# Key loads moved from SyncE's hardware queue to GpSimd's software queue, and state rows the other way

## The chip, the core and the metric

The kernel runs on one core of one Trainium2 chip. The core's engines work side by side: TensorE (PE in the profile, its weight loads PEld), VectorE (DVE), ScalarE (ACT), GpSimd (POOL) and SyncE (SP). SP computes nothing here; it only starts data transfers. Transfers run on 16 shared DMA engines. A transfer started by SP goes through queue q1, whose descriptors are made in hardware; one started by GpSimd goes through queue q0, whose descriptors GpSimd writes in software (the page calls the two kinds "hardware_dynamic" and "software_dynamic"). The metric is device time in microseconds (us) of the one core, taken without the profiler; the profile is one execution of its own.

## What is computed

For 16 sequences of 2048 steps with 256 channels, the reference runs this recurrence for every channel. It is the numerically safe form of a weighted mean over the past, with decay `w` per step and a bonus `u` for the current step:

```python
for t in range(seq_len):
    kk = k[b, t, :].copy()
    vv = v[b, t, :].copy()
    ww = u + kk
    qq = np.maximum(pp, ww)
    e1 = np.exp(pp - qq)
    e2 = np.exp(ww - qq)
    output[b, t, :] = (e1 * aa + e2 * vv) / (e1 * bb + e2 + 1e-08)
    ww = pp - w + kk
    qq = np.maximum(ww, kk)
    e1 = np.exp(ww - qq)
    e2 = np.exp(kk - qq)
    aa = e1 * aa + e2 * vv
    bb = e1 * bb + e2
    pp = qq
```

`k`, `v` and the output have 16 x 2048 x 256 float32 numbers, 33.55 MB each.

## The kernel before

The time axis is cut into a head of 32 steps and 16 stages of 126 steps. In a stage, the steps lie on the partitions and the recurrence becomes matrix products with triangular matrices. The unit of work is a **pair**: four sequences of one stage, 126 steps x 4 x 256 numbers. There are 64 such pairs (16 stages x 4), and two smaller ones for the head, which are put third and fourth: 66 pairs in all, numbered n = 0 to 65.

One pair takes these operations, by line:

- `load` (L121; L115 for the head): one transfer of 512 KB for `k` into a tile `kr` and one for `v` into a tile `vr`. Each tile has four buffers.
- `round_k` (L258, DVE): casts `kr` into `km`, a float32r matrix that also holds rows with `w` and `u`. `logs` (L266, PE): `km` times two matrices gives the exponents X in PSUM. `exps` (L277, ACT): their exponentials, into the tile `ez`.
- `cast_v` (L285, DVE): `vr` to bfloat16 `vb`. `times_v` (L293, DVE): `ez` times `vb`.
- `sums` (L323, PE): sums over the steps of a stage, for the state.
- `den` (L457, PE), `recip` (L465 and L466, ACT), `num` (L475, PE), `mult` (L483, DVE): denominator, its reciprocal, numerator, and the product, into the tile `rd`.
- `store` (L499, GpSimd; L494 for the head): one transfer of 504 KB from `rd` to the output.

Once per stage, a chain of small operations carries the state from stage to stage (L332 to L424; on DVE among others the copy of the sums L346, the copy L364, then L366 to L368, L387 to L392, L402, L404 and L417). It ends in `inject`: DVE copies the new state into a small tile `row` (L429), and four transfers of 8 KB put it into partitions 126 and 127 of the `ez` tiles of that stage (L433, issued by GpSimd), where the `den` and `num` of the stage's pairs read it.

The main loop has one **slot** per pair, and the order of work on every engine is written out by hand: a helper `K` pins each instruction behind the one before it on its engine. Slot n issues the load of pair n + 3, then the exponentials of pair n, `round_k` of pair n + 1, the output work (`num`, `den`, `recip`, `mult`) of pairs ten or eleven slots back with the store, `times_v` of pair n, `logs` and `cast_v` of pair n + 1. A stage's state is injected at the end of the third slot after its last pair, three slots before the first `den` that reads it. After the last pair, eleven slots only finish outputs.

SP has nothing else to do than loads, in the order k, v, k, v, so it runs ahead of the slots: each load starts as soon as its buffer is free, and a buffer is free when the cast that reads it (`round_k` or `cast_v`) has ended four pairs earlier. GpSimd does its setup work in the first microseconds and afterwards only issues stores and state rows; it waits for the second `mult` of a pair before its store.

Of the kernel before, what the change touches and what calls it, by code (L numbers as in the profile page):

```python
# [22 lines left out]
def kernel(  # L23
# [11 lines left out]
    def K(ins):  # L35

        block, e, new = nc.cur_bb.bb, ins.ins.engine, []
        for i in reversed(block.instructions):
            if i.engine == e:
                new.append(i)  # L40
                if i.name == pinned.get(e):
                    break
        for a, b in zip(new[1:], new):
            tc.add_manual_dep(b, a.name, mybir.DependencyInfo(
                mybir.DependencyClass.NoSync, mybir.DependencyReason.DATA), reason="order")
        pinned[e] = new[0].name
        return ins

    PE, DVE, SC, POOL, SP = nc.tensor, nc.vector, nc.scalar, nc.gpsimd, nc.sync
# [3 lines left out]
    TC = 2 * HS  # L53
# [3 lines left out]
    GB = T0  # L57
    NG = 3
    NH = NG * GB
    AHEAD = 3  # L60
    LAG = 10
    RS = 2.0 ** -43
    LNRS = 43 * 0.6931471805599453
    CAP = 68.0

    consts = ctx.enter_context(tc.tile_pool(name="consts", bufs=1))
    kpool = ctx.enter_context(tc.tile_pool(name="kpool", bufs=AHEAD + 1))
    vpool = ctx.enter_context(tc.tile_pool(name="vpool", bufs=AHEAD + 1))
    vbpool = ctx.enter_context(tc.tile_pool(name="vbpool", bufs=2))
    ezpool = ctx.enter_context(tc.tile_pool(name="ezpool", bufs=7))  # L70
    rpool = ctx.enter_context(tc.tile_pool(name="rpool", bufs=5))
# [15 lines left out]
    NP = len(pairs)  # L87
    kr_of, vr_of = {}, {}

    def is_head(n):  # L90
        return pairs[n][0] < 0

    def tiles_of(n):
        return 1 if pairs[n] == (-1, 1) else 2
# [6 lines left out]
    def load(n):  # L101
        kr = kpool.tile([128, 4, Dm], F32, tag="kr", name="kr")
        vr = vpool.tile([128, 4, Dm], F32, tag="vr", name="vr")
        kr_of[n], vr_of[n] = kr, vr
        c, p = pairs[n]
        if is_head(n):
            if p == 1:
                K(POOL.memset(kr[64:96, 0:2, :], 0.0))
                K(POOL.memset(vr[64:96, 0:2, :], 0.0))
            for t, x in ((kr, k), (vr, v)):  # L110
                for g in range(NG):
                    b = 6 * g + 4 * p
                    e = min(b + 2 * tiles_of(n), B)
                    if b < e:
                        K(SP.dma_start(out=t[g * GB:(g + 1) * GB, 0:e - b, :],  # L115
                                        in_=x[b:e, 0:T0, :].rearrange("n t d -> t n d")))
        else:
            t0 = T0 + c * TC
            r = min(128, T - t0)
            for t, x, eng in ((kr, k, SP), (vr, v, SP if n else SC)):  # L120
                K(eng.dma_start(  # L121
                    out=t[0:r, :, :], in_=x[4 * p:4 * p + 4, t0:t0 + r, :].rearrange("n t d -> t n d")))

# [5 lines left out]
    for n in range(2):  # L129
        load(n)  # L130
# [54 lines left out]
                               -0.5 * HS, op=ALU.mult))  # L185
    fill(NLE[0:HS, TC:TC + 1], 0.5)
    K(DVE.scalar_tensor_tensor(NLE[:, TC + 1:128], cc[:, 2:3], -0.5 * HS, cc[:, 4:5], ALU.mult, ALU.add))
    for n in range(2, AHEAD + 1):
        load(n)
    kms = [consts.tile([128, 4, Dm], F32R, tag=f"km{j}", name=f"km{j}") for j in range(2)]  # L190
    for t in kms:
# [55 lines left out]
    EZ, X_of, KM = {}, {}, {}  # L247

    def round_k(n):
        r = NH if is_head(n) else TC  # L250
        i = 2 * tiles_of(n)
        if is_head(n):
            KM[n] = rpool.tile([128, 2, D], F32, tag="rd", name="kmh").rearrange(
                "p i (n d) -> p (i n) d", n=2).bitcast(F32R)
            K(SC.activation(KM[n][96:98], crow[96:98], ACT.Copy))
        else:
            KM[n] = kms[n % 2]
        K(DVE.tensor_copy(KM[n][0:r, 0:i, :], kr_of.pop(n)[0:r, 0:i, :]))  # L258
# [14 lines left out]
    def exps(n):  # L273
        if n % 2 == 0:
            EZ[n // 2] = ezpool.tile([128, 4, 4, D], BF16, tag="ez", name="ez")
        i = tiles_of(n)
        K(SC.activation(ez_of(n)[:, 0:4:2], X_of.pop(n)[:, :, 0:i, :], ACT.Exp))  # L277
# [26 lines left out]
    def group_of(c, j):  # L304
        return 2 * j if c == 0 else 1 + 2 * c + j
# [6 lines left out]
    def sums(n):  # L312
        c = step_of(n)
        head = c < 0
        if n == first_of[c]:
            TOT[c] = psn.tile([128, D], F32, tag="num", name="num")[0:48] if head else pst.tile(
                [48, D], F32, tag="tot", name="tot")
        for i in range(tiles_of(n)):
            for q in range(2):
                x = 2 * pairs[n][1] + i  # L320
                m = ((OHE, OHV), (OHhE, OHhV))[head][q][:, 8 - x:56 - x]
                r = (NH + NG if head else 128) if q == 0 else (NH if head else TC)
                K(PE.matmul(TOT[c], m[0:r, :], ez_of(n)[0:r, q, i, :],  # L323
                            start=n == first_of[c] and i == 0 and q == 0,
                            stop=n == last_of[c] and i == tiles_of(n) - 1 and q == 1,
                            skip_group_check=True))
# [100 lines left out]
    def inject(c):  # L427
        row = small.tile([128, 128], BF16, tag="row", name="row")
        K(DVE.tensor_copy(row, st.pop((c, "d"))[:, 0:128]))  # L429
        for j in range(2):  # L430
            for h in range(2):
                p = 64 * h + 32 * j
                K(POOL.dma_start(out=EZ[group_of(c, j)][TC + h:TC + h + 1, 0:2, :, :].rearrange(  # L433
                                   "o q i (x c) -> o (q i x) c", c=128),
                               in_=row[p:p + 32, :]))

# [5 lines left out]
    def widen():  # L442
        first_phase.close()
        for name, bufs in (("den", 1), ("num", 2)):
            wide.append(ctx.enter_context(tc.tile_pool(name="wide" + name, bufs=bufs, space=bass.MemoryType.PSUM)))
# [6 lines left out]
    def den(n):  # L452
        rl, ri = (NH, NH) if is_head(n) else (128, TC)
        d = bank("den", [128, 2, D])
        for m, r, q in (((Lh if is_head(n) else Lf), rl, 0), (Id, ri, 2)):
            for i in range(tiles_of(n)):
                K(PE.matmul(d[:, i, :], m[0:r, :], ez_of(n)[0:r, q, i, :], start=q == 0, stop=q == 2,  # L457
                            skip_group_check=True))
        DEN[n] = d

    def recip(n):
        r = NH if is_head(n) else TC
        i = tiles_of(n)
        rd = rpool.tile([128, 2, D], F32, tag="rd", name="rd")
        K(SC.activation(rd[0:r, 0:i, :], DEN.pop(n)[0:r, 0:i, :], ACT.Ln, scale=RS))  # L465
        K(SC.activation(rd[0:r, 0:i, :], rd[0:r, 0:i, :], ACT.Exp, scale=-1.0))  # L466
        RD[n] = rd

    def num(n, i):
        if i >= tiles_of(n):  # L470
            return
        rl, ri = (NH, NH) if is_head(n) else (128, TC)
        d = bank("num", [128, D])
        for m, r, q in (((LhN if is_head(n) else LfN), rl, 1), (IdN, ri, 3)):
            K(PE.matmul(d, m[0:r, :], ez_of(n)[0:r, q, i, :], start=q == 1, stop=q == 3,  # L475
                        skip_group_check=True))
        NUM[n, i] = d

    def mult(n, i):
        if i >= tiles_of(n):  # L480
            return
        r = NH if is_head(n) else TC
        K(DVE.tensor_mul(RD[n][0:r, i, :], NUM.pop((n, i))[0:r, :], RD[n][0:r, i, :]))  # L483
# [34 lines left out]
    def small_work(n, where):  # L518
        for f, c in later.pop((n, where), []):
            f(c)  # L520
# [12 lines left out]
    for n in range(NP + LAG + 1):  # L533
        q, qp = out_at.get(n), out_at.get(n - 1)
        live, out_q, out_qp = n < NP, q is not None, qp is not None
        if n == NP:
            widen()
        if 0 < n and n + AHEAD < NP:
            load(n + AHEAD)
        small_work(n, "first")  # L540
        if live:
            exps(n)
        small_work(n, "exp")
        if 0 < n <= NP:
            sums(n - 1)
        if n + 1 < NP:
            round_k(n + 1)
        small_work(n, "sums")
        if out_qp:
            num(qp, 0)  # L550
            if not live:
                num(qp, 1)
        if out_q:
            den(q)
            recip(q)
        if out_qp:
            mult(qp, 0)
            if live:
                num(qp, 1)
        small_work(n, "pool")  # L560
        if live:
            times_v(n)
        if out_qp:
            mult(qp, 1)
            store(qp)
        if n + 1 < NP:
            logs(n + 1)
            cast_v(n + 1)
        small_work(n, "dve")
        small_work(n, "act")  # L570
        small_work(n, "last")
# [31 lines left out]
```

## Time and profile before

Five runs of the kernel: 350.89, 352.67, 353.19, 353.79 and 355.10 us, median 353.19. The profiled execution is the slowest of them.

| | profiled execution |
|---|---|
| its own time | 355.10 us |
| its span, first to last instruction | 353.4 us |
| DVE busy | 297.1 us, 84% |
| PE busy | 289.5 us, 82% |
| ACT busy | 278.7 us, 79% |
| POOL busy | 99.7 us, 28% |
| stores L499 on POOL | 64, mean 916 ns each |
| state rows L433 on POOL | 64, mean 520 ns each |
| store, issue to landing | median 7.5 us |
| state row, issue to landing | median 7.1 us |
| read from and written to HBM | 68.22 MB and 33.55 MB |

How to read it: "busy" counts the time in which an engine executed something. GpSimd's busy time here is the time in which it writes descriptors, not the transfer itself. The kernel has three phases. It starts up until about 80 us (the pipeline of ten slots fills), it then repeats a steady pattern of four slots, one stage, every 18.66 us until about 310 us, and it drains until 353 us. In a timeline line of the profile, the columns are start in us, length in us, engine, line, operation, tile written <- tiles read, and count.

### The profile page before, as it was taken

The page shows a single profiled execution, that of the slowest core. Times are in us where ns is not written, and L with a number is a line of the kernel's source. Part 1 is how long each engine was busy: PE and PEld are TensorE (multiplying, and loading weights), DVE is VectorE, ACT ScalarE, POOL GpSimd, SP SyncE. Part 2 cuts the span into 40 slices and gives each one's busy share as a digit, 9 for nine tenths or more (in the row PEclk, how much of TensorE's full clock was granted, in tenths as well). Part 3 has the DMA queues.
Part 4 walks back from the last instruction along what each step waited for, and adds up shares of the span by engine and source line. Part 5 has one row for each costly group of instructions (what it writes and reads, how often), then busy time and mean ns, then how long its engine had stood idle before and what let it go on. Part 6 is the DMA issues. An engine that isn't in the chain of part 4 may idle for free.

```text
span 353.4 us, 4174 instructions
## 1 busy us (share of the span) xinstructions
PE 289.5 (82%) x1183; PEld 139.4 (39%) x1200; DVE 297.1 (84%) x636; ACT 278.7 (79%) x286; POOL 99.7 (28%) x164
## 2 busy tenths in 40 slices
PE   0568877788979898988989898979797989887970
PEld 0225433343435444444444353535343544433320
DVE  2566787889999999999999999999999999986451
ACT  2474557779988889898989898888988889977790
POOL 5000006131414141514132231405141405142531
PEclk9975889999999999999999999999999999999895
DMA  7898768699999999999999999999999999634574
GB/s 213 198 352 279 221 224 249 205 326 301 311 354 332 369 313 366 304 360 317 355 328 340 354 334 330 329 336 337 345 335 350 319 313 287 200 123 148 182 237 138
DMA packets 81366, 102.59 MB, mean 290 GB/s; under 512 B 5504, under 2 KB 73152, under 8 KB 81344
## 3 DMA queue, kind: packets, MB, share of 16 engines
q1 hardware_dynamic: 68160, 67.58, 60.2%
q0 software_dynamic: 12496, 34.11, 27.8%
q10 hardware_dynamic: 688, 0.66, 0.8%
q8 instruction: 9, 0.15, 0.2%
q14 instruction: 13, 0.11, 0.1%
HBM read 68.22 MB, written 33.55 MB: 288 GB/s over the span
## 4 chain that ended last, share of the span: by engine, by line
PE 38%; DVE 27%; issue 5%; DMA 4%; ACT 2%; POOL 0%; POOLq 0%; DVEq 0%
PE num L475 11%; PE X L266 9%; DVE rd L483 8%; PE den L457 7%; PE tot L323 7%; DVE ez L293 5%; DVE km L258 4%; DMA ez<-row 4%; PE den L339 4%; DVE vb L285 2%; DVE AB L392 2%; DVE da L391 1%; DVE S L366 1%; ACT rd L466 1%; ACT rd L465 1%
## 5 line engine op out<-in xcount | busy, mean ns | idle before, releaser
L277 ACT ACTIVATE ez<-X 128x2048 bf16<-128x2048 f32 x66 | 122.2, 1852 | 23.4 <-PE X L266 23.4
L499 POOL DMA_DIRECT2D out_dram<-rd x64 | 58.6, 916 | 197.4 <-DVE rd L483 69.5
L483 DVE TENSOR_TENSOR rd<-num,rd 126x512 f32<-126x512 f32 (+1 forms) x131 | 88.5, 682 | 14.5 <-ACT rd L466 7.0
L293 DVE TENSOR_TENSOR ez<-ez,vb 126x2048 bf16<-126x2048 bf16 (+1 forms) x66 | 79.7, 1208 | 8.0 <-ACT ez L277 6.6
L465 ACT ACTIVATE rd<-den 126x1024 f32<-126x1024 f32 (+1 forms) x66 | 66.7, 1011 | 20.7 <-PE den L457 20.7
L466 ACT ACTIVATE rd<-rd 126x1024 f32<-126x1024 f32 (+1 forms) x66 | 69.5, 1053 | 2.1
L266 PE MATMUL X<-km,NLE 128*128 128x512 f32 x128 | 54.4, 508 | 16.2 <-DVE km L258 13.1
L475 PE MATMUL num<-ez,LfN 128*128 128x512 bf16 x127 | 49.0, 386 | 21.4 <-DVE rd L483 20.8
L323 PE MATMUL tot<-ez,OHV 126*48 126x512 bf16 x128 | 49.8, 389 | 8.5 <-DVE ez L293 8.5
L258 DVE CAST km<-kr 126x1024 fp32r<-126x1024 f32 x64 | 50.6, 790 | 5.0 <-ACT km L192 5.0
L323 PE MATMUL tot<-ez,OHE 128*48 128x512 bf16 x128 | 50.8, 397 | 0.0
L475 PE MATMUL num<-ez,IdN 126*128 126x512 bf16 (+1 forms) x131 | 50.3, 384 | 0.2 <-issue 0.2
L285 DVE CAST vb<-vr 126x1024 bf16<-126x1024 f32 (+1 forms) x66 | 44.6, 676 | 3.3 <-DMA vr<-in_v_dram 3.3
L433 POOL DMA_DIRECT2D ez<-row x64 | 32.9, 520 | 47.1 <-DVE km L258 47.1
L266 PE MATMUL X<-km,NLZ 128*128 128x512 f32 x128 | 42.1, 412 | 0.0
L457 PE MATMUL den<-ez,Id 126*128 126x512 bf16 (+1 forms) x131 | 40.0, 386 | 0.9
L266 PEld LDWEIGHTS X<-km,NLE 128*128 128x128 f32 x128 | 24.9, 202 | 29.7 <-DVE km L258 10.0
L457 PE MATMUL den<-ez,Lf 128*128 128x512 bf16 x112 | 35.1, 383 | 1.3 <-DMA ez<-row 1.3
L475 PEld LDWEIGHTS <-IdN 126*128 126x128 bf16 (+1 forms) x131 | 12.8, 98 | 40.4 <-issue 39.2
L266 PEld LDWEIGHTS X<-km,NLZ 128*128 128x128 f32 x128 | 25.7, 201 | 6.2
L323 PEld LDWEIGHTS <-OHE 128*48 128x48 bf16 x128 | 13.2, 103 | 32.8 <-issue 25.7
L475 PEld LDWEIGHTS <-LfN 128*128 128x128 bf16 x128 | 12.4, 97 | 31.7 <-issue 23.2
(95 smaller groups left out, 199.7 us busy)
## 6 DMA issues: line engine op xcount, KB each, us to landing
out_dram<-rd POOLq DMA_DIRECT2D x64, 504.0 KB, 7.5
kr<-in_k_dram SPq DMA_DIRECT2D x60, 512.0 KB
vr<-in_v_dram SPq DMA_DIRECT2D x59, 512.0 KB
kr<-in_k_dram SPq DMA_DIRECT2D x4, 504.0 KB
vr<-in_v_dram SPq DMA_DIRECT2D x4, 504.0 KB
ez<-row POOLq DMA_DIRECT2D x64, 8.0 KB, 7.1
vr<-in_v_dram ACTq DMA_DIRECT2D x1, 512.0 KB
kr<-in_k_dram SPq DMA_DIRECT2D x3, 128.0 KB
```

Source lines behind the costliest of these rows:

```text
L258: K(DVE.tensor_copy(KM[n][0:r, 0:i, :], kr_of.pop(n)[0:r, 0:i, :]))
L266: K(PE.matmul(X[:, q, i, :], m[0:kr, :], km[0:kr, i, :], start=True, stop=True))
L277: K(SC.activation(ez_of(n)[:, 0:4:2], X_of.pop(n)[:, :, 0:i, :], ACT.Exp))
L285: K(DVE.tensor_copy(vb[0:r, 0:i, :], vr_of.pop(n)[0:r, 0:i, :]))
L293: K(DVE.tensor_mul(ez[0:r, 1:4:2], ez[0:r, 0:4:2], vb[0:r, 0:i, :].unsqueeze(1).broadcast_to([r, 2, i, D])))
L323: K(PE.matmul(TOT[c], m[0:r, :], ez_of(n)[0:r, q, i, :], start=n == first_of[c] and i == 0 and q == 0, stop=n == last_of[c] and i == tiles ...
L457: K(PE.matmul(d[:, i, :], m[0:r, :], ez_of(n)[0:r, q, i, :], start=q == 0, stop=q == 2, skip_group_check=True))
L465: K(SC.activation(rd[0:r, 0:i, :], DEN.pop(n)[0:r, 0:i, :], ACT.Ln, scale=RS))
L466: K(SC.activation(rd[0:r, 0:i, :], rd[0:r, 0:i, :], ACT.Exp, scale=-1.0))
L475: K(PE.matmul(d, m[0:r, :], ez_of(n)[0:r, q, i, :], start=q == 1, stop=q == 3, skip_group_check=True))
L483: K(DVE.tensor_mul(RD[n][0:r, i, :], NUM.pop((n, i))[0:r, :], RD[n][0:r, i, :]))
L499: K(POOL.dma_start(out=out[4 * p:4 * p + 4, t0:t0 + TC, :].rearrange("n t d -> t n d"), in_=o[0:TC, :, :]))
```

## The change

The loads of `k` are issued by GpSimd instead of SP, from pair 5 on. The loads of `v` stay on SP. The four transfers of state rows per stage are issued by SP instead of GpSimd. The load of a pair is written four slots ahead of the pair instead of three; the number of buffers stays at four (it was `AHEAD + 1` with `AHEAD = 3` and is `AHEAD` with `AHEAD = 4`). Pairs 0 to 3 are loaded before the loop, as before; pair 4 is now loaded in slot 0 instead of slot 1.

```diff
-    AHEAD = 3
+    AHEAD = 4
...
-    kpool = ctx.enter_context(tc.tile_pool(name="kpool", bufs=AHEAD + 1))
-    vpool = ctx.enter_context(tc.tile_pool(name="vpool", bufs=AHEAD + 1))
+    kpool = ctx.enter_context(tc.tile_pool(name="kpool", bufs=AHEAD))
+    vpool = ctx.enter_context(tc.tile_pool(name="vpool", bufs=AHEAD))
...
-            for t, x, eng in ((kr, k, SP), (vr, v, SP if n else SC)):
+            for t, x, eng in ((kr, k, SP if n <= AHEAD else POOL), (vr, v, SP if n else SC)):
                 K(eng.dma_start(
                     out=t[0:r, :, :], in_=x[4 * p:4 * p + 4, t0:t0 + r, :].rearrange("n t d -> t n d")))
...
-    for n in range(2, AHEAD + 1):
+    for n in range(2, AHEAD):
         load(n)
...
-                K(POOL.dma_start(out=EZ[group_of(c, j)][TC + h:TC + h + 1, 0:2, :, :].rearrange(
+                K(SP.dma_start(out=EZ[group_of(c, j)][TC + h:TC + h + 1, 0:2, :, :].rearrange(
                                    "o q i (x c) -> o (q i x) c", c=128),
                                in_=row[p:p + 32, :]))
...
-        if 0 < n and n + AHEAD < NP:
+        if n + AHEAD < NP:
             load(n + AHEAD)
```

The instructions of PE, DVE and ACT and their order stay as they were. On GpSimd, the order from pair 4's output on becomes: store, k load, store, k load. On SP, it becomes: four v loads, four state rows, four v loads.

## The prediction

> **What bounds the kernel now.** I read the 40-slice rows first, then busy time by stretch, then the waits, then DVE against POOL in the timeline. The page:
>
> ```profile
> DVE  2566787889999999999999999999999999986451
> ...
> DMA  7898768699999999999999999999999999634574
> ...
> q1 hardware_dynamic: 68160, 67.58, 60.2%
> q0 software_dynamic: 12496, 34.11, 27.8%
> ```
>
> Two resources are at 9 from about 80 to 300 us: DVE and the DMA engines. Busy time by stretch, columns stretch, length, busy time of PE, PEld, DVE, ACT, POOL with counts, granted clock, DMA share, GB/s:
>
> ```profile
> 20.00:80.00 60.00, 48.57 (x172) 24.12 (x174) 45.03 (x103) 37.94 (x41) 10.18 (x15) 0.83 0.82 262
> 105.00:305.00 200.00, 180.70 (x776) 88.41 (x787) 191.64 (x386) 178.40 (x182) 62.05 (x87) 1.00 1.00 333
> ```
>
> In the steady part DVE works 191.6 of 200 us and the DMA share reads 1.00. Which one binds? The list of waits of the whole span decides (engine, line, releaser: us in total, times, longest):
>
> ```profile
> DVE vb L285 <- DMA vr<-in_v_dram: 3.3, 1, 3.3
> ...
> PE den L457 <- DMA ez<-row: 1.3, 1, 1.3
> ```
>
> DVE waits for a load once, for the first v; between 105 and 305 us its only listed wait is 2.8 us before L483. So DVE's instruction stream sets the 18.66 us per stage, and transfers are hidden. By how much: counting completion packets of q1 in the trace dates each load's landing. k of pair 25 was issued at 105.21, landed at 109.50 and was cast at 122.82 us; in the steady part k lands 11 to 15 us early. The chain of waits does give 4% (14 us) to "DMA ez<-row", but at both places (75.6 and 91.4 us) the instruction it releases follows other work on its engine without a gap; I give these 14 us no weight.
>
> Now DVE beside POOL in one stage:
>
> ```profile
> 122.53 0.81 POOL L499 DMA_DIRECT2D out_dram<-rd  x1 [5.49 <-DVE rd L483]
> 127.01 1.15 POOL L499 DMA_DIRECT2D out_dram<-rd  x1 [3.67 <-issue]
> 128.15 2.03 POOL L433 DMA_DIRECT2D ez<-row  x4
> 130.78 0.91 POOL L499 DMA_DIRECT2D out_dram<-rd  x1 [0.61 <-DVE vb L285]
> 134.86 0.83 POOL L499 DMA_DIRECT2D out_dram<-rd  x1 [3.17 <-ACT rd L466]
> ```
>
> ```profile
> 122.82 1.00 DVE L258 CAST km<-kr 126x1024 fp32r<-126x1024 f32 x1
> ...
> 127.15 0.68 DVE L258 CAST km<-kr 126x1024 fp32r<-126x1024 f32 x1
> ...
> 130.68 0.68 DVE L258 CAST km<-kr 126x1024 fp32r<-126x1024 f32 x1
> ...
> 134.94 0.36 DVE L346 COPY tsum<-den 128x192 f32<-128x192 f32 x1
> 135.21 0.97 DVE L258 CAST km<-kr 126x1024 fp32r<-126x1024 f32 x1
> 136.10 0.16 DVE L364 COPY S<-S 128x32 f32<-128x32 f32 x1
> ```
>
> The same cast takes 0.68 us, or 1.00 and 0.97. It is long exactly when it starts 0.29 to 0.37 us after a store begins on POOL; when it starts at -0.10 or +0.14, the cast keeps its 0.68 and the store stretches to 0.91 or 1.15. All stages repeat this; in start-up a cast at +0.25 and +0.27 still won. I read it as one shared thing, taken by a store from about +0.28 to +0.63 us of its own time, or, after having waited for a cast, for about 0.24 us. Operations with a PSUM operand (L483) and L293 run beside POOL at their usual 0.68 and 1.21 us. I call the stage's four slots A, B, C, D by their store: A and D cost DVE 0.3 us each.
>
> **The change part by part.**
>
> *Order on POOL.* A k load sits directly behind the store of the slot before. Its buffer has been free since that slot's L258, and its place in GpSimd's eight completion semaphores was last used four slots (18.7 us) ago, against a longest store landing of 9.1; so it starts when the store ends. POOL loses 64 rows (64 x 0.52 = 33 us) and gains 61 loads; a load has the store's shape (128 x 4 rows of 1 KB against 126 x 4), so 0.81 us free, 49 us. POOL goes from 28% to about 33%, and the next store comes over 3 us after: no cost by itself.
>
> *Collisions with DVE.* The stores keep their distance from the second L483 (0.58 us), and DVE's order is unchanged, so A and D should lose 0.3 us as before. The load's own window: in A and D it starts at +0.81, asks at +1.09, while the delayed cast runs to about +1.3; it waits, then holds about 0.24 us. In A the cast is followed by L483, in B and C the load falls on L483 and L293: nothing is lost. In D the cast is followed by L364, a float32 copy inside SBUF. That L364 obeys the same exclusion rests on one instance, the only one beside a store: at 319.77 us, 0.62 after the store's start, it took 0.19 instead of 0.16 us. Bounds per stage: 0 (L364 slips through) to 0.35; I take 0.23, nearest to the stores that waited. Twelve D slots lie between 80 and 310 us: 12 x 0.23 = **+2.8 us** (0 to +4.2).
>
> Here a rule speaks against the change harder than the trace. The Trainium skill, "SBUF — State Buffer", section "SBUF: two separate sides", says that DVE and GpSimd lock a shared port pair, and whoever starts first keeps it for the whole instruction. By the rule, the store at 122.53 would hold the cast at 122.82 until 123.34, 0.52 us; the trace shows 0.32. If the load held its whole 0.81 us behind the cast, D would cost 0.8 per stage, +9.7 us. The measured row decides; the rule's figure stays as the upper end.
>
> *State rows on SP.* Each row's issue and the rows' landing shift. SP waits at the rows for DVE's L429; queued behind are v loads, whose buffers free at about the same time; four rows at 0.39 us (the last head loads on SP) delay one v load per stage by 1.6 us, against 13 us of slack. The one real wait for rows is at 59.16 us, where PE's `den` stood 1.29 us. There the row was cast by 52.78 us; on SP four issues end at 54.4, and a load issued then on q1 landed in 2.2 to 2.7 us, so rows land by 57.1, before 57.87 when PE is ready. PE and ACT set the pace there and DVE idles 2.03 us behind them: **-1.3 us**, between 0 and -1.8. The next wait is then PE's `num` for L483. Three slots of cover (14 us) hide later rows.
>
> *k loads in start-up.* Sixteen k loads (pairs 5 to 20) go through POOL before 90 us, each up to 0.35 us of a cast: 0 to 5.6 us. About a third of DVE's time there is casts, 16 x 1/3 x 0.24 = 1.3, and DVE is 75% busy (45.0 of 60): **+1.0 us**.
>
> *Landing of k.* k now starts behind the store: pair 25 at about 109.5 instead of 105.21, so 13.3 us before its cast, less 0.8 for descriptors. A store's median landing is 7.5 us, longest 9.1; queued behind a store's packets (128 x 159 ns / 16 = 1.3 us) about 10.4. Slack about 2 to 3 us: hidden, at no cost. Without it each us of lateness recurs every three slots, over 47 slots 16 us.
>
> *DMA engines.* In q0 a 4 KB packet took 159 ns, in q1 1 KB took 46, 184 per 4 KB. If k loads travel in 4 KB packets, 25 ns per 4 KB go: the steady share falls from 0.965 (packet times summed, 118 to 155 us) to about 0.92. Bounds: 184 ns (no relief) and no gain of time either way, since nothing waits on loads. It would cost only above 203 ns, where the share passes 1. Four pairs ahead with the same four buffers changes nothing: buffers, not slots, release v.
>
> **Sum** against the profiled span of 353.4: +2.8 - 1.3 + 1.0 = +2.5, 355.9. That execution (355.1) was the slowest of five with median 353.19; on the median's scale 353.2 + 2.5 = **355.7 us**, +0.7%. Differences under about 1% are what a measurement of this kernel can't tell from none.
>
> **Rivals.**
>
> *Every load costs DVE (slower).* A load in slot A, C or B also catches a cast or small copy, or holds for its whole length. Place: L258 and L364. It decides once loads start later than +0.2 us behind the store's end, or hold beyond 0.35 us. Price: 0.8 per stage by the rule, +9.7 - 1.3 + 1.0 = +9.4, 362.6; 0.3 for each of 47 loads, +14, 367. For: the 1.00 us casts. Against: L483 and L293 follow, which rows on POOL never slowed.
>
> *k lands late (slower).* Place: DVE waits at L258; from 12.5 us of landing. At 0.5 us over: +8 + 2.5, 363.7. For: DMA share 1.00. Against: 7.5 us stores.
>
> *The knife edge tips (faster).* In A the cast starts at +0.29 and loses, at +0.27 it won. If POOL starts stores 0.02 us later, A wins back 0.32 per stage: 13 x 0.32 = 4.2. With -1.3 and no hit on L364: 347.7. For: the margin. Against: POOL's 0.58 us from L483 to store is constant whatever preceded.
>
> *The change does nothing*: L364 slips through, the start-up terms cancel: 353.
>
> **How the numbers follow.** Forecast with the last case, 0.58 (own range 352.5 to 358.5; 0.39 of it below 356.7, within 1%, 0.17 above, 0.02 faster). Each load costs DVE, 0.17, slower. k late, 0.08, slower. Knife edge, 0.17, faster. So faster 0.19, within 1% 0.39, slower 0.42. Range 348.5 to 363.0: it leaves out the lower third of the knife edge and the upper halves of the two slower rivals.
>
> **What would show it.** L258 still 1.00 in A and D, 0.68 in B and C; L364 at about 0.4 in D; store and load back to back on POOL; PE's wait for `ez<-row` gone; no DVE wait for `kr`; q0 packets of 4 KB for k. Wrong if L258's mean moves off 790 ns by over 50, or L258 waits for a transfer.

## The result

| | before | changed |
|---|---|---|
| median of all runs | 353.16 us (48 runs, 350.17 to 356.94) | 350.86 us (27 runs, 346.34 to 353.78) |
| profiled execution, its own time | 355.10 us | 352.07 us |
| its span | 353.4 us | 350.4 us |
| length of a steady stage (L346 to L346, median of twelve) | 18.66 us | 18.52 us |
| L258, mean of 64 | 790 ns | 741 ns |

The changed kernel is faster by 1.3%: the ratio is 0.9873, 95% interval 0.9849 to 0.9896. The ratio leaves out runs over 1.5% above the fastest of their own kernel, which are 13 of the changed kernel's 27 (and its profiled execution) but one of the 48 before, so it favours the change; the medians of all runs alone give 0.9935. A second measurement of both kernels (the first experiment) gave 0.993, interval 0.9907 to 0.9953. The gain is real, and lies between 0.5 and 1.5%.

The page of the changed kernel, the rows that answer to those of before (busy tenths of DVE, clock granted to PE, share of the DMA engines in 40 slices; then the queues: packets, MB, share):

```profile
DVE  2666777889999999999999999999999999987451
...
PEclk9995669999999999999999999999999999999896
DMA  7899664799999999999999999999999999943675
...
q0 software_dynamic: 19296, 65.53, 54.6%
q1 hardware_dynamic: 39064, 36.15, 33.3%
...
L121 POOL DMA_DIRECT2D kr<-in_k_dram x61 | 48.2, 790 | 38.1 <-DVE km L258 23.8
...
L258 DVE CAST km<-kr 126x1024 fp32r<-126x1024 f32 x64 | 47.4, 741 | 4.7 <-ACT km L192 4.7
```

The k loads are in q0 now, 61 of them, and write descriptors for 790 ns each. DVE still stands at 9 in the steady part. The bound has not moved. The last row has the surprise: the mean of the cast fell by 49 ns, where my forecast had it unchanged (and over 50 as a sign of being wrong). Busy time by stretch, columns as in the prediction:

```profile
105.00:305.00 200.00, 181.92 (x782) 89.27 (x792) 191.49 (x391) 180.09 (x184) 76.70 (x85) 1.00 1.00 338
```

DVE is as busy as before (191.5 of 200 us, 191.6 before), and does 391 instructions in that time in place of 386. Its instructions became shorter, not its idle time. In the list of waits of the whole span, DVE's wait for `vr` is there as before, PE's wait for `ez<-row` is gone, and DVE has none for `kr`:

```profile
DVE vb L285 <- DMA vr<-in_v_dram: 3.1, 1, 3.1
```

In what follows a cast **wins** when it keeps its 0.68 to 0.69 us beside a transfer that POOL writes, and **loses** when it takes longer. Now the same stage as in the prediction, POOL and then DVE (start, length, engine, line):

```profile
122.12 1.28 POOL L499 DMA_DIRECT2D out_dram<-rd  x1 [4.92 <-issue]
123.39 0.77 POOL L121 DMA_DIRECT2D kr<-in_k_dram  x1
126.29 1.12 POOL L499 DMA_DIRECT2D out_dram<-rd  x1 [2.13 <-ACT rd L466]
127.40 0.77 POOL L121 DMA_DIRECT2D kr<-in_k_dram  x1
130.02 0.92 POOL L499 DMA_DIRECT2D out_dram<-rd  x1 [1.86 <-ACT rd L466]
130.93 0.77 POOL L121 DMA_DIRECT2D kr<-in_k_dram  x1
134.09 0.83 POOL L499 DMA_DIRECT2D out_dram<-rd  x1 [2.39 <-ACT rd L466]
134.91 0.80 POOL L121 DMA_DIRECT2D kr<-in_k_dram  x1
```

```profile
122.02 0.18 DVE L402 TENSOR_SCALAR m<-y 128x64 f32<-128x64 f32 x1
122.24 0.23 DVE L404 SCALAR_TENSOR_TENSOR m<-S,m 128x64 f32<-128x64 f32 x1
122.38 0.69 DVE L258 CAST km<-kr 126x1024 fp32r<-126x1024 f32 x1
...
126.39 0.68 DVE L258 CAST km<-kr 126x1024 fp32r<-126x1024 f32 x1
...
129.92 0.69 DVE L258 CAST km<-kr 126x1024 fp32r<-126x1024 f32 x1
...
134.19 0.36 DVE L346 COPY tsum<-den 128x192 f32<-128x192 f32 x1
134.46 0.95 DVE L258 CAST km<-kr 126x1024 fp32r<-126x1024 f32 x1
135.34 0.36 DVE L364 COPY S<-S 128x32 f32<-128x32 f32 x1
```

Slot A is at 122. Its cast starts 0.27 us after its store and takes 0.69, where it started 0.29 after and took 1.00; the store is now the one that waits (1.28 instead of 0.81). In slot D, at 134, the cast is long as before, and L364 behind it takes 0.36 instead of 0.16, because the k load at 134.91 is being written beside it. Of twelve stages, eleven have the short cast in A, and ten the long L364 in D. Worked out in nanoseconds from the trace, as medians over the twelve stages:

| | before | changed |
|---|---|---|
| slot A: second L483 to start of store | 1268 | 1295 |
| slot A: store to cast; length of the cast | +295; 1005 | +269; 685 |
| slot D: second L483 to start of store | 1312 | 1297 |
| slot D: store to cast; length of the cast | +355; 968 | +375; 953 |
| slot D: length of L364 | 161 | 361 (160 in two stages) |

So a stage gains 0.32 us in A and pays 0.20 in D. The span's 3.0 us divide like this, by the first and last L346 of the steady part: 0.5 before 97 us, 1.2 from there to 318 us, 1.3 in the drain. The 0.5 and the 1.3 are not to be relied upon: the drains (from the last L346 on) of two almost equal kernels below, two forms of one nudge, took 33.7 and 30.9 us.

### The profile page after: what moved, and what is told of

Read it like the earlier page. It is cut to its first block, busy times and chain, and to the rows that moved or that the text cites. A ratio compares the mean times of both kernels' runs of the same rounds, so it can differ in the third digit from the quotient of the medians.

```text
span 350.4 us, 4111 instructions
## 1 busy us (share of the span) xinstructions
PE 291.6 (83%) x1183; PEld 140.1 (40%) x1200; DVE 296.5 (85%) x636; ACT 279.3 (80%) x286; POOL 119.4 (34%) x161
## 4 chain that ended last, share of the span: by engine, by line
PE 50%; DVE 32%; ACT 8%; issue 4%; DMA 3%; ACTq 0%; POOLq 0%; DVEq 0%
PE X L266 15%; PE num L475 13%; PE tot L323 9%; PE den L457 9%; DVE rd L483 8%; PE den L339 5%; DVE km L258 5%; DVE ez L293 5%; ACT ez L277 4%; DMA vr<-in_v_dram 3%; DVE vb L285 3%; DVE AB L392 2%; ACT rd L465 2%; DVE da L391 2%; DVE S L366 2%
## 5 line engine op out<-in xcount | busy, mean ns | idle before, releaser
L499 POOL DMA_DIRECT2D out_dram<-rd x64 | 63.6, 994 | 178.5 <-issue 73.2
L483 DVE TENSOR_TENSOR rd<-num,rd 126x512 f32<-126x512 f32 (+1 forms) x131 | 88.8, 684 | 15.1 <-ACT rd L466 7.0
L293 DVE TENSOR_TENSOR ez<-ez,vb 126x2048 bf16<-126x2048 bf16 (+1 forms) x66 | 79.9, 1210 | 7.3 <-ACT ez L277 5.9
L121 POOL DMA_DIRECT2D kr<-in_k_dram x61 | 48.2, 790 | 38.1 <-DVE km L258 23.8
L323 PE MATMUL tot<-ez,OHV 126*48 126x512 bf16 x128 | 51.2, 400 | 8.3 <-DVE ez L293 8.3
L323 PE MATMUL tot<-ez,OHE 128*48 128x512 bf16 x128 | 52.3, 409 | 0.0
L258 DVE CAST km<-kr 126x1024 fp32r<-126x1024 f32 x64 | 47.4, 741 | 4.7 <-ACT km L192 4.7
L285 DVE CAST vb<-vr 126x1024 bf16<-126x1024 f32 (+1 forms) x66 | 44.7, 678 | 3.1 <-DMA vr<-in_v_dram 3.1
```

What stands on the lines that cost most here:

```text
L285: K(DVE.tensor_copy(vb[0:r, 0:i, :], vr_of.pop(n)[0:r, 0:i, :]))
L293: K(DVE.tensor_mul(ez[0:r, 1:4:2], ez[0:r, 0:4:2], vb[0:r, 0:i, :].unsqueeze(1).broadcast_to([r, 2, i, D])))
L323: K(PE.matmul(TOT[c], m[0:r, :], ez_of(n)[0:r, q, i, :], start=n == first_of[c] and i == 0 and q == 0, stop=n == last_of[c] and i == tiles ...
L499: K(POOL.dma_start(out=out[4 * p:4 * p + 4, t0:t0 + TC, :].rearrange("n t d -> t n d"), in_=o[0:TC, :, :]))
```

## The experiments

Eleven kernels, each measured beside the kernel before. Ratios are to the kernel before. Line numbers of edited kernels are shifted, so L258 is named "the cast" where they differ.

**1. The changed kernel again.**

> The changed kernel once more, with a new profile. Theory L (lock): what counts is who comes first, the store on POOL or the cast L258 on DVE. In slot A the cast keeps 0.68 us (it was 1.00 before the change), and in slot D the copy L364 takes 0.36 us (it was 0.16), so a stage takes 18.66 - 0.32 + 0.20 = 18.5 us; a stage in which L364 escapes takes 18.3. If executions of one kernel differ by several us, L expects different stage periods in them. Rival C (clock): the periods are alike and the executions differ in start-up, before 97 us, where the granted clock dips. Ratio to the kernel before 0.985 to 0.995 by both.

Measured 351.08 us (22 runs, 347.25 to 354.74), ratio 0.993 (0.9907 to 0.9953). The cast takes 686 ns in A and 958 in D, L364 362, the stage 18.54 us. The pattern belongs to the kernel, not to one execution.

**2. Only k on GpSimd.** The changed kernel with the rows back on GpSimd.

```diff
-                K(SP.dma_start(out=EZ[group_of(c, j)][TC + h:TC + h + 1, 0:2, :, :].rearrange(
+                K(POOL.dma_start(out=EZ[group_of(c, j)][TC + h:TC + h + 1, 0:2, :, :].rearrange(
```

> Only the k loads go to GpSimd; the state rows stay on GpSimd. Theory L: casts in slot A at 0.68 us if it is the k load that makes the store start 0.03 us later, L364 at 0.36 us, stages at 18.5 us; the 1.3 us wait of PE for rows near 59 us stays: ratio 0.992 to 0.997. Rival D (larger packets relieve the DMA engines): the whole gain stays, 0.987. Rival R (the rows on SP make the gain): nothing is left, 1.000, or slower by the 2.4 us of L364, 1.007.

Measured 348.81 us, ratio 0.9901 (0.9864 to 0.9938). A's store starts 1277 ns after the second L483, the cast at +287, and it wins in 11 of 12 stages. D is mixed: five of twelve casts at 685, and L364 between 161 and 495. The stages take 18.28 to 18.56 us, the last 18.83. The part with the k loads is enough for the gain, and the shortened casts in A go with it. The ratio is below what theory L gave (0.992 to 0.997); the five short casts in D may be the rest, which no run takes apart.

**3. Only the rows on SP.** The kernel before with that line turned the other way, everything else as it was (three pairs ahead).

> Only the state rows go to SP; k stays on SP, three pairs ahead with four buffers as before. Theory L: L364 stays at 0.16 us; the wait of 1.3 us near 59 us is gone; slot A's cast stays at 1.00 if the k load sets the store's start (ratio 0.996), or drops to 0.68 if the rows' absence from GpSimd sets it (another 12 x 0.32 = 3.8 us, ratio 0.985). Rival R: 0.987 without any change of L258. Rival D: 1.000.

Measured 357.03 us, ratio 1.0109 (1.0065 to 1.0153), slower. From the waits of its whole span, SP's queue and DVE:

```profile
SPq L433 <- DVE row L429: 96.6, 16, 14.0
```

```profile
DVE km L258 <- DMA kr<-in_k_dram: 6.5, 5, 2.9
```

SP reaches the rows early and stands there for L429, up to 14 us, with all k and v loads queued behind. DVE then waits for k, 6.5 us in five places, and stages of 19 to 20 us appear among those of 18.6. The cast in A keeps its 1.00 us in eight of twelve stages, with its store 1270 ns after the second L483. No expectation had this kernel slower: the queue behind the rows was overlooked.

**4 and 5. Nudges in slot A.** The changed kernel, with a memset on DVE ahead of L402, of 2 and of 64 columns, to move the cast of A back.

```diff
+    nudge = consts.tile([128, 64], F32, tag="nudge", name="nudge")
...
+        K(DVE.memset(nudge, 0.0))
```

> The changed kernel with one more DVE instruction per stage, a memset of two columns (0.06 us) ahead of L402 in slot A, so that the cast L258 starts about 0.33 instead of 0.27 us after the store. Theory L: the cast loses, takes 1.00 us again, and each of 12 stages costs 0.06 + 0.32 us, +4.6 us against the changed kernel: ratio to the kernel before about 1.000. Rivals D and R: only 16 x 0.06 = 1 us, ratio 0.990.

> The changed kernel with a wider extra DVE memset (64 columns) ahead of L402 in slot A, since the two-column one moved the cast L258 by only 0.01 us. Theory L: the cast now starts about 0.33 us after the store, loses, takes 1.00 us again; a stage takes 18.5 + 0.07 + 0.32 = 18.9 us, 12 of them cost 4.7 us against the changed kernel, ratio to the kernel before about 1.005. Rivals D (packets) and R (rows): only the memset, 16 x 0.07 = 1.1 us, ratio 0.995.

Measured 351.51 us, ratio 0.9951 (0.992 to 0.9982), and 350.58, ratio 0.9932 (0.991 to 0.9954). Both missed: the memset of 64 columns ran almost wholly beside L402 (from the start of L285 to that of L404 it took 0.84 us instead of 0.82), the cast came at +277 and +283 ns, and stayed at 686 in A in 11 and in 10 of 12 stages; the three that lost started at +294 to +311. They don't test the lock as meant, and only say that its edge lies above +283.

**6. The knife edge alone, no transfer touched.** In the kernel before, L404 of slot A is written behind the cast.

```diff
+        st[c, "m1"] = m
+
+    def inject_cap(c):
+        m = st.pop((c, "m1"))
...
-                     (s + 2, "act", inject_logs), (s + 3, "first", inject_min), (s + 3, "exp", inject_weights),
+                     (s + 2, "act", inject_logs), (s + 3, "first", inject_min), (s + 3, "sums", inject_cap), (s + 3, "sums", inject_weights),
```

> The kernel before, with one DVE operation of slot A (L404) moved from ahead of the cast L258 to behind it; no transfer is touched. Theory L: the cast starts about 0.15 us after the store instead of 0.29, wins, takes 0.68 instead of 1.00; 12 stages x 0.32 = 3.8 us, ratio 0.989, stages at 18.3 us. Rivals D and R: 1.000, or slower if ScalarE waits for the later L404.

Measured 346.55 us (345.1 to 348.58), ratio 0.9838 (0.9797 to 0.9879): below both kernels. A's store and DVE's stream there, from the timeline:

```profile
120.58 1.05 POOL L503 DMA_DIRECT2D out_dram<-rd  x1 [5.49 <-DVE rd L487]
```

```profile
120.51 0.19 DVE L402 TENSOR_SCALAR m<-y 128x64 f32<-128x64 f32 x1
120.61 0.69 DVE L258 CAST km<-kr 126x1024 fp32r<-126x1024 f32 x1
121.21 0.22 DVE L408 SCALAR_TENSOR_TENSOR m<-S,m 128x64 f32<-128x64 f32 x1
```

The cast starts 0.03 us after the store (0.15 was expected), takes 0.69 in all twelve stages, and the store pays (1.05). The stage takes 18.22 us, 0.44 less: 0.32 is the cast, and 0.12 is L402, behind which L404 no longer has to wait (L402 to the next instruction: 0.10 instead of 0.22 us). Moving one small instruction brings more than the whole change of the transfers.

**7. No descriptor writing beside a cast.** The changed kernel, with each k load written behind its slot's cast and each store behind that load.

```diff
+        if AHEAD < n + AHEAD < NP and n > 0:
+            load_k(n + AHEAD)
...
+        if late:
+            store(late.pop())
...
-            store(qp)
+            if n + 2 < NP:
+                late.append(qp)
+            else:
+                store(qp)
```

> The changed kernel with GpSimd's order turned: the k load is written directly behind L258 of the pair whose buffer it takes over, and the store of the slot before behind that load, so that both begin about 0.6 us after a cast and end before the next one. Theory L: every L258 takes 0.68 us, L364 takes 0.16, a stage takes 18.66 - 0.32 - 0.29 = 18.05 us; against the changed kernel 12 x 0.45 = 5.4 us, ratio to the kernel before 0.975 to 0.980. Rivals D and R: as the changed kernel, 0.987 to 0.993.

Measured 347.53 us, ratio 0.9842 (0.9804 to 0.988). The cast takes 0.68 to 0.69 us in all four slots until the loads end, L364 0.17. The stage is 18.27, not the 18.05 expected. Setting DVE's stages side by side, instruction by instruction, shows the rest: L483 in slot D is followed by the next instruction (L387) after 0.79 us instead of 0.60. DVE comes there 0.28 us earlier and gives 0.19 back. The list of waits doesn't name the cause, but the timeline does (lines are shifted by 16: L383 is L367, L391 is L375, L403 is L387):

```profile
133.95 0.77 POOL L136 DMA_DIRECT2D kr<-in_k_dram  x1 [2.94 <-DVE S L380]
...
134.30 0.41 DVE L383 TENSOR_SCALAR ex<-S 128x64 f32<-128x64 f32 x1
...
135.01 0.30 ACT L391 ACTIVATE g<-ex 128x128 f32<-128x128 f32 x1
...
135.34 0.29 DVE L403 TENSOR_TENSOR tb<-tsum,g 128x128 f32<-128x128 f32 x1
```

The k load, moved out of the way of the cast and of L364, now falls on L367: 0.35 us into the load it takes 0.41 us instead of 0.19. ScalarE makes `g` from its result that much later, and L387, which reads `g`, starts 0.03 us after `g` is done (0.18 in the changed kernel). So this order is not quite free of collisions.

**8. All loads and the rows on SP, four pairs ahead.** The changed kernel with the k loads on SP again.

```diff
-            for t, x, eng in ((kr, k, SP if n <= AHEAD else POOL), (vr, v, SP if n else SC)):
+            for t, x, eng in ((kr, k, SP), (vr, v, SP if n else SC)):
```

> The changed kernel with all k loads on SP: rows on SP, loads written four pairs ahead with four buffers. E3 (rows on SP, loads written three ahead) was slower; if that is because SP stood at the rows with loads of earlier need behind them, it is gone here: no DVE wait for kr. Theory L: nothing else changes in the steady part (slot A 1.00, D 0.97, L364 0.16, stages 18.66), ratio 0.996 to 1.000. Rival R: 0.990. If rows on SP cost by themselves: over 1.005.

Measured 350.91 us, ratio 0.9947 (0.9921 to 0.9974), 6 us below experiment 3 although only the distance of the loads differs. SP's queue in the list of waits:

```profile
SPq L433 <- DVE row L429: 80.9, 16, 14.5
```

SP stands at the rows for about as long. But the loads that DVE needs next were written a slot earlier and are ahead of the rows, and no wait of DVE for `kr` is left. A's cast is at 1004 ns (no k load on POOL, the edge not crossed), D's at 901, and the stage takes 18.58. The ratio is slightly better than theory L's 0.996 to 1.000. This matters for the change: a kernel whose cast in A loses is level with the changed one by the medians of all runs (350.86, and 351.08 in experiment 1) and by experiment 1's ratio (0.993), though not by the first ratio of 0.9873. Start-up is shorter (17.63 us from the second L346 to the third, 19.08 before), and without rows on POOL the store of D starts 1268 ns after the second L483 instead of 1312, so the cast there loses 0.07 us less. Rows on SP with the loads four pairs ahead may thus bring about as much as the whole change; k on GpSimd adds the win in A and the loss at L364.

**9. A nudge that can't slip aside.** The changed kernel with one more small operation in slot A that needs L404's result.

```diff
         K(DVE.scalar_tensor_tensor(m2, st[c, "S"][:, 0:2, :], 0.0, m, ALU.max, ALU.min))
+        K(DVE.tensor_scalar(m2, m2, 1.0, 0.0, ALU.mult, ALU.add))
```

> The changed kernel with one more small operation on VectorE in slot A (the 128x64 result of L404 multiplied by 1 in place, so it waits for L404), which should move the cast by 0.13 to 0.22 us against A's store; the output is unchanged. Lock theory: the cast of A starts 0.40 to 0.49 us after its store instead of 0.27, falls into the stretch that the store holds (to about 0.63) and takes about 0.80 to 0.92 instead of 0.69, and the next operation of DVE starts no earlier than about 0.63 + 0.60 us after the store; so a stage is 0.32 to 0.36 us longer than the changed kernel's, more than the added operation alone, 12 times, about +4 us: 355. Rival, that the cast of A became short because k travels through GpSimd's queue or because less goes through the DMA engines, not because of where the store falls: it stays at 0.69 us and the stage grows by the added operation alone, 0.13 to 0.22, +2 us: 353.

Measured 356.77 us, ratio 1.0113 (1.007 to 1.0156), slower than both. The timeline of POOL and of DVE in slot A:

```profile
123.12 0.83 POOL L500 DMA_DIRECT2D out_dram<-rd  x1 [4.93 <-issue]
```

```profile
123.24 0.23 DVE L404 SCALAR_TENSOR_TENSOR m<-S,m 128x64 f32<-128x64 f32 x1
123.50 0.44 DVE L405 TENSOR_SCALAR m<-m 128x64 f32<-128x64 f32 x1
123.61 0.87 DVE L258 CAST km<-kr 126x1024 fp32r<-126x1024 f32 x1
```

L405 starts 0.38 us after the store and takes 0.44; the cast behind it starts 0.49 us after the store and takes 0.87. The store is back at its free 0.83: it lost nothing. k travels through GpSimd's queue in this kernel as in the changed one, so the queue and the packets alone don't keep the cast short. The stage takes 18.93 us, 0.41 more; the added operation alone explains about 0.22 of it (the distance from L402 to L404, two such operations in a row).

**10. The change, with slot A out of the way.** The edit of experiment 6 on top of the changed kernel.

> The changed kernel with L404 of slot A written behind L258 (the same edit that took 0.45 us per stage off the kernel before and brought it to 346.6). With slot A out of the lock in both, what is left between the two is the change without its knife edge. My theory (the gain of the change in slot A is the knife edge, and apart from it the change costs 0.20 per stage at L364 and gains 0.5 in start-up and 1.3 in the drain): stage 18.41 (18.53 less 0.12), and +2.4 - 1.8 = +0.6 against that kernel, 347 us, slower than 346.6 or level with it. Rival, that the loads of k on GpSimd and their larger packets bring the gain themselves: the same 2.3 us below that kernel, 344.3, stage near 18.08.

Measured 347.2 us, ratio 0.9827 (0.9785 to 0.9869), stage 18.41 us. Against experiment 6 (0.9838, stage 18.22) that is level: the stage is 0.19 longer (L364 again at 361 ns), and rows and the ends of the kernel make up for it. The rival needed 344.3, a ratio of 0.975, which lies outside the interval. Without the knife edge the change is worth nothing that these runs can tell: what the rows on SP gain, the k loads lose.

**11. Both.** Experiment 7 with the edit of experiment 6.

> The changed kernel with each k load written behind its slot's cast, each store behind that load (as in the quiet version, 347.5 us), and L404 of slot A behind L258. Nothing on GpSimd starts beside a cast any more. Theory: of the 0.45 us that moving L404 brought in the kernel before, 0.32 was the lock, which the quiet version already has; the other 0.12 was L404 waiting for L402, and it comes here too: stage 18.26 - 0.12 = 18.14, 12 times, 346.1 us. Rival, that both edits bring different things and add up: stage 17.8, 342 us.

Measured 345.56 us (342.02 to 345.76), ratio 0.9762 (0.9723 to 0.98), the lowest of all. POOL in slot D and the slot after it, and DVE in slot D:

```profile
114.54 0.77 POOL L136 DMA_DIRECT2D kr<-in_k_dram  x1 [2.91 <-DVE S L380]
115.31 0.83 POOL L519 DMA_DIRECT2D out_dram<-rd  x1
```

```profile
113.29 0.36 DVE L362 COPY tsum<-den 128x192 f32<-128x192 f32 x1
113.57 0.68 DVE L272 CAST km<-kr 126x1024 fp32r<-126x1024 f32 x1
114.16 0.17 DVE L380 COPY S<-S 128x32 f32<-128x32 f32 x1
```

GpSimd starts to write when cast and copy are through (L383, which is L367, is caught here too: 0.41 us). The stage is 18.14 us, just what the theory gave: the two edits don't add up, since both take the same 0.32 us out of slot A.

## Why the prediction was wrong

The time, 350.9, lies in the range, but I forecast 355.7 and most of the chance on no gain. Term by term:

- **The bound, and the lock: right.** DVE's stream sets the stage, the transfers are hidden, and what the cast loses depends on where it starts against a store. Experiments 6 and 9 show this from both sides: the same cast at +32 ns takes 0.69, at +494 ns, behind L405 which had waited first, 0.87.
- **"The stores keep their distance from the second L483 (0.58 us), so A and D should lose 0.3 us as before": the step that failed.** I called the distance constant whatever preceded. Counted from the end of L483 it was 585 ns (medians) in A and B, but 629 in C and D already before the change; with a k load ahead of each store it is 613 in all four. In A that moves the store 27 ns later and the cast from +295 to +269. The traces of both kernels and of all experiments but 9, taken together, show how near the edge that was: all 65 casts that started 200 to 288 ns after a store won, all 125 at 297 to 430 ns lost, and of the 30 in between five won. I had named this as a rival and then dismissed it on a reading coarser than its margin. Its price, 347.7, left the hit on L364 and the start-up loads out; with the forecast's own terms for both (+2.8 and +1.0) it would have been 351.5. The mean of A's twelve casts fell from 979 to 711 ns (one of twelve falls out of the pattern in either kernel): 12 x 0.27 = 3.2 us.
- **L364 beside the load in slot D, +2.8: right, a little large.** 0.20 per stage in ten of twelve stages, 2.0 us. In A, B and C the loads cost DVE nothing, as forecast: L483 beside them keeps 0.68 and L293 1.22. The stricter rule's +9.7 (the lock held for the whole 0.81 us) did not come.
- **Rows on SP, -1.3: right, where the clock lets it be seen.** PE's wait for `ez<-row` is gone. In the changed kernel's own profile that stretch is no shorter, though (19.07 us from the second L346 to the third, 19.08 before). Busy time by stretch over it, before, changed, and experiment 9, which has the changed transfers; the column before the last two is the granted clock:

```profile
43.00:53.00 10.00, 7.67 (x27) 3.73 (x27) 8.22 (x24) 6.25 (x9) 0.00 (x0) 0.83 0.62 203
53.00:63.00 10.00, 8.05 (x38) 4.08 (x36) 7.00 (x11) 7.29 (x9) 5.46 (x9) 1.00 0.84 265
```

```profile
43.00:53.00 10.00, 7.60 (x22) 3.33 (x21) 7.64 (x22) 5.43 (x9) 1.50 (x2) 0.71 0.65 197
53.00:63.00 10.00, 9.34 (x40) 4.59 (x40) 7.83 (x13) 8.20 (x10) 4.80 (x7) 0.95 0.54 174
```

```profile
43.00:53.00 10.00, 7.61 (x26) 3.43 (x24) 8.52 (x24) 6.09 (x9) 1.50 (x2) 0.83 0.67 204
53.00:63.00 10.00, 9.34 (x43) 4.74 (x43) 8.28 (x17) 8.75 (x10) 4.99 (x7) 1.00 0.66 200
```

  PE works 9.34 of the second ten us in place of 8.05: it no longer waits. But in the changed kernel's profile the granted clock was 0.71 and 0.95 there. With the clock of before (0.83 and 1.00) experiment 9 needs 17.75 us, 1.33 less. The other profiles with rows on SP divide in the same way: 17.62 to 17.75 us in those at 0.83 and 1.00 (experiments 3, 7, 8 and 11), 19.03 to 19.12 in those below (1, 4, 5 and 10). That the clock is the cause is read from this agreement; no run sets it.
- **k loads in start-up, +1.0: too large.** The same stretch takes 17.63 us in experiment 8 (k on SP) and 17.75 in experiment 9 (k on GpSimd), both at 0.83 and 1.00: 0.1 us. One small operation (L367, 0.35 us into a k load at 44.10 us in experiment 9) took 0.39 instead of 0.19.
- **k's landing, 7.5 to 10.4 us, hidden: right.** The median is 7.6, the last four take 11.0, and DVE waits for none.
- **Relief of the DMA engines, 0.965 to 0.92: wrong, without effect.** q0 and q1 together take 87.9% of the span, 88.0% before. It was to bring no time in any case.
- **"Four pairs ahead changes nothing": wrong as a general statement.** With all loads on SP and the rows there too, three pairs ahead give 357.0 and four 350.9. In the changed kernel, where only v stands behind the rows, it wasn't tried.

With the right sign in A the sum would have been -3.2 + 2.0 - 1.3 + 0.1 = -2.4 us, 350.8 on the median's scale, against 350.86 measured. That it fits to a tenth is luck: the two measured ratios leave room for a gain of 1.7 to 5.3 us. That the store moved to the good side of the edge, and not away from it, was luck too.

What stays open: why the store's start depends on what POOL writes besides stores. In the steady part of experiments 3 and 8, where POOL writes stores alone, it is 585 ns after L483 in all four slots; in the kernel before it is 629 in C and D, the two stores behind the rows; with k loads between the stores it is 613. No run takes the cause apart. The 1.3 us of the drain can't be told from its variation.

## What to carry to other kernels

When two engines share something and who goes first decides, read both starts in nanoseconds over all repetitions before calling a distance constant: here a margin of about 10 ns, crossed by accident, was worth 0.3 us in each stage, 3.2 us in all, where the whole kernel gained 1.7 to 5.3. Such a gain should be taken on purpose, by the order of instructions: one small operation moved behind the cast brought 346.6, descriptors written right after the cast 347.5, and both together 345.6 us. The first kept its short cast on the changed kernel too (experiment 10, at +6 ns, far from the edge). Descriptors moved out of one operation's way can fall on the next, as L367 shows. And a queue that is given an issue which waits for an engine needs whatever is behind it to be written early enough: the rows on SP cost 1.1% with loads three pairs ahead and nothing with four.

## What the runs showed of the hardware

The edge between winning and losing is narrow: in twelve traces every cast that started 200 to 288 ns after the start of a store on GpSimd's queue won, every one at 297 to 430 ns lost, and between 289 and 296 ns five won and 25 lost. The loser waits until about 0.62 to 0.64 us of the store's time (the cast's start plus what it took over 0.685: 295 + 320 and 355 + 283 ns), not until the store's end at 0.81. Small float32 operations inside SBUF take part as the casts do: L364 went from 161 to 361 ns, L367 beside a k load from 0.19 to 0.41 us, and the added 128x64 operation of experiment 9, 0.38 us after the store, took 0.44. And the granted clock in start-up moves without a cause that these runs show: from 43 to 53 us it was 0.79, 0.69 and 0.83 in the profiled executions of experiments 4, 5 and 9, which differ by one small instruction, and the stretch around it took 19.07, 19.12 and 17.75 us.
